# In a two-block kernel's second block, VectorE makes the weights' low parts, ScalarE the high parts and the MLP's squares

## The chip, the cores and the metric

The kernel runs on one core of one Trainium2 chip. The metric is the device time of one execution, in microseconds. The kernel before takes 1734.81 us, the median of 3 runs (1733.33 to 1739.93).

## The reference

256 tokens of width 1024, all in fp32, pass through two blocks. The first has two layers: a gated linear attention and an mLSTM, each followed by a mixture of 16 experts. The change leaves it alone. The second block, cut to its core:

```python
c_act = silu(c)
for l in range(2):
    ada = c_act @ w_ada[l] + b_ada[l]                 # 1024 x 6144: six modulation vectors
    sh1, sc1, gt1, sh2, sc2, gt2 = split(ada, 6)
    h = rms(x, g_mix[l]) * (1 + sc1) + sh1
    parts = split(h @ w_in[l], IN_SPLITS)             # q, k, v of both attentions, and two gates
    y_a = gqa_attention(rope(rms(qa)), rope(rms(ka)), va) @ w_branch_a[l]      # 8 heads over 2
    y_b = dilated_attention(rope(rms(qb)), rope(rms(kb)), vb) @ w_branch_b[l]  # 3 groups of 4 heads
    mixed = sigmoid(gate_a) * y_a + sigmoid(gate_b) * y_b
    x = x + gt1 * (mixed @ w_out[l])
    h2 = rms(x, g_mlp[l]) * (1 + sc2) + sh2
    x = x + gt2 * (square(relu(h2 @ w_ff1[l])) @ w_ff2[l])     # 1024 -> 4096 -> 1024
```

## The kernel before, in words

**Split weights.** A product in fp32 is made of three matmuls: a matrix is split into a high part (`hi`, a cast to a shorter format) and a low part (`lo`, the matrix less its high part), and TensorE adds high by high, high by low and low by high. Activations are split the same way, once (`X_H` and `X_L`; in the MLP `fh` and `fl`). The weights come from HBM in units of 1 MB; half a unit is a chunk of 128 x 1024, and `split` (L349 to L365) makes one chunk's `hi` and `lo`. It is called `LOOK` = 2 chunks ahead of the chunk that TensorE multiplies by (`ahead`), and there are 4 buffers of each kind. A few chunks are split earlier, at the end of a stage (`early`), with `lo` on GpSimd.

**Who makes what.** The Python program that writes the instructions carries a planner. `Clock` (L107) keeps an estimated time of each engine and the estimated end of everything read or written; its cost table (`Timed.cost`) gives each operation a duration by engine and size, and knows nothing of one engine slowing another. `Either` takes, of two engines, the one whose estimated end is earlier, after a handicap: `AV` chooses ScalarE or VectorE (0.0); `VG` VectorE or GpSimd, with GpSimd taken where it would end less than 0.5 us after VectorE; `VG2` the same two, with GpSimd taken only where it would end over 1.0 us earlier. Before the change `hi` goes by `AV`, `lo` by `VG`. Each engine then works off its own instructions in the order in which the program wrote them.

**The second block, layer by layer.** The input projection is followed by the attentions: heads normalised and rotated (`norm_rope`; the result is `xs`, and the small powers of the norms, `hss`, are GpSimd's), scores, softmax, values. The branch projections and gates give `mixed`, transposed and split. The output projection (`out_proj`, L649) works through 128 of the 256 tokens first (mt=0), then the other 128. After each half and 512 columns `emit` (L2300) multiplies by `gt1` (`res`), adds to the residual (`h`), and takes ScalarE's sum of squares (`aff_q`). With a half done, the norm for the MLP starts in the background: `th` is the modulated norm, `X_H` and `X_L` its parts. The MLP (`mlp`, L2317) goes in 8 blocks of 512 hidden columns. `dense_T` leaves a block transposed in PSUM, `square_T` (L2331) makes the relu (`r`), its square, and `fh` and `fl`, two pieces of 128 x 512 for each block; the first block takes another way (`up`, `turn`; there `fl` is taken from PSUM, `fl<-tp,fh`). `down` multiplies the block before by `w_ff2`.

**The modulation columns.** `ada_cols` (L1848) is a generator that runs in the background of other stages, a step at each tick. For each layer it makes 12 groups of 512 columns; each group takes 4 loads of 512 KB (`ada_w`, two buffers). For a load, ScalarE scales one half by `c` (`ada_t`), VectorE multiplies and adds the other half (the load's buffer is then free, and the next load goes out), and from the second load on an addition joins it to the group's sum. After the fourth, VectorE transposes and reduces (`part`), and TensorE finishes with four tiny matmuls (`bgp<-part,fold`), which are taken from a list of hooks at certain places. Two things hold the generator back: a schedule by chunks (`CB`), and `calm` (L1944), which puts a step off, up to ten times, while the planner's clock has the step's engine over 0.9 us later than TensorE. `ada_need(l, 9)` in `emit`, called at the end of the first token half, makes sure that the group 9 is done, the last one that the MLP's norm uses: it takes hooks and ticks until it is.

All operations are recorded by one helper, so that every row of the profile has the line L175; operations are told apart by their tiles.

Of the kernel before, what the change touches and what calls it, by code (L numbers as in the profile page):

```python
# [26 lines left out]
F32 = mybir.dt.float32  # L27
# [3 lines left out]
AF = mybir.ActivationFunctionType  # L31
OP = mybir.AluOpType
# [195 lines left out]
def tile_model(ctx: ExitStack, tc: tile.TileContext, I, out, stages=None, h_in=None):  # L228
    nc = tc.nc
    clock = Clock()  # L230
    PE, V, A, G = [Timed(clock, e, n) for e, n in
                   ((nc.tensor, "PE"), (nc.vector, "V"), (nc.scalar, "A"), (nc.gpsimd, "G"))]
    SP = Timed(clock, nc.sync, "D")
    copies = {("V", "copy"): "tensor_copy"}
    VG, AV = Either((V, G), -0.5), Either((A, V), 0.0, copies)
    VG2 = Either((V, G), 1.0)
# [31 lines left out]
    class Stream:  # L268
# [80 lines left out]
        def split(self, i):  # L349
            u, half = self.chunks[i]  # L350
            shape = self.units[u][0]
            while u not in self.tiles:
                B.tick()
            t = self.tiles[u]
            n = shape[1] // 2
            src = t[:, half * n:half * n + n]
            src = src.rearrange("p k n -> p (k n)")
            hi = clock.slot("hi", 4, hl.tile([P, 1024], F32R, name="hi", tag="hi"))
            lo = clock.slot("lo", 4, hl.tile([P, 1024], F32R, name="lo", tag="lo"))
            AV.copy(hi, src)  # L360
            (G if self.pool else VG).tensor_tensor(lo, src, hi.bitcast(F32), op=OP.subtract)
            self.ready[i] = (hi, lo)
            if half:
                self.tiles.pop(u)
                self.free(u)  # L365
# [651 lines left out]
    def moe_front(l, space):  # L1017
# [99 lines left out]
        def front(mt, nb, rs, norm):  # L1117


            if nb == 0:  # L1120
                if mt == 0:

                    A.activation(R["top0"], c_ones[:, 0:1], AF.Sigmoid)
                B.push(first(mt), True)
            elif mt == 0:
                B.push(later(rs, norm), True)
            else:
                B.drain()
                split(0)
                part(1, 1)  # L1130
                norm()
                logits(1, 1)
                for _ in sigmoids(1, rs):
                    pass
                split(1)
# [1181 lines left out]
    def mlp(l, x, mp):  # L2317
# [13 lines left out]
        def square_T(pq, f):  # L2331
            for i in range(2):
                yield
                r = mp.tile([P, 2, T], F32, name="r", bufs=2)
                A.activation(r, pq[i], AF.Relu)
                VG2.tensor_tensor(r, r, r, op=OP.mult)
                k = slice(2 * i, 2 * i + 2)
                AV.copy(f.hi[:, k], r)
                VG2.tensor_tensor(f.lo[:, k], r, f.hi[:, k].bitcast(F32), op=OP.subtract)

        def turn(r, f):
            yield 1
# [34 lines left out]
        for fb in range(8):  # L2377
            f = XT(mp.tile([P, 4, T], F32R, name="fh", bufs=2), mp.tile([P, 4, T], F32R, name="fl", bufs=2))
            if fb:
                B.push(square_T(dense_T(x), f), True)  # L2380
            else:
                B.push(turn(up(fb), f), True)
            if fb == 6:
                B.push(ada_row(l, 1, gt, 1.0), True)
            if fb:
                down(fb - 1, fx[-1])
            fx.append(f)
# [35 lines left out]
    src = h_in if h_in is not None else I["x"][0]  # L2423
# [240 lines left out]
```

## Time and profile before

| of the profiled execution | |
|---|---|
| span | 1732.9 us |
| its own device time | 1734.7 us |
| TensorE busy (PE) | 1576.5 us, 91% |
| weight loads (PEld) | 1136.3 us, 66% |
| VectorE busy (DVE) | 1112.8 us, 64% |
| ScalarE busy (ACT) | 574.2 us, 33% |
| GpSimd busy (POOL) | 395.3 us, 23% |
| `lo` on GpSimd | 104, mean 2548 ns |
| `lo` on VectorE | 204, mean 1287 ns |
| `hi` on ScalarE | 207, mean 1050 ns |

The second block lies between about 860 and 1720 us. The first layer's output projection adds its residual (`res`) from 1076 to 1088 us, its MLP from 1293 us on; in the second layer the two lie at 1518 to 1528 us and at the end, 1721 us. The attentions' heads come at the start of each layer, round 885 and 1335 us. An engine's busy time is the sum of its instructions' durations, and an instruction that is slowed down by another engine counts with its longer duration. "PEclk" is the clock that TensorE was granted, as a share of the full 2.4 GHz; its other level is 1.2 GHz. "mean ns of one" is a group's mean, and what stands behind the bar is the time in which the engine was idle ahead of the group's instructions, with what ended most of it.

### The profile page before, as it was taken

To read this page: it belongs to the slowest core of one execution; us is meant where nothing else is said; L and a number is where in the kernel's file an instruction comes from. 1 tells how busy PE (TensorE), PEld (TensorE's weight loads), DVE (VectorE), ACT (ScalarE), POOL (GpSimd) and SP (SyncE) were. 2 spreads that over 40 slices of the span, in tenths; PEclk is the share of its full clock that TensorE was granted. 3 is DMA by queue.
4 is the path that set the end of the run, shared out by engine and by line. 5 is a ranking of instruction groups with operands and counts; after the bars stand their busy time and mean duration, and the time that the engine had idled before them with its cause. 6 is when DMAs were issued, how large, how long until landed. Compare 5 with 4: busy or idle time off the path is not lost.

```text
span 1732.9 us, 22647 instructions
## 1 busy us (share of the span) xinstructions
PE 1576.5 (91%) x8772; PEld 1136.3 (66%) x8774; DVE 1112.8 (64%) x1728; ACT 574.2 (33%) x973; POOL 395.3 (23%) x256
## 2 busy tenths in 40 slices
PE   7998999898998799989788998888998889989997
PEld 5865444336776544433466897778986679878996
DVE  4876113106887611121498979898889987779875
ACT  5223111105543211201344453533434544352210
POOL 1232000001333100000364324432125531222110
PEclk9998999898999899999998999999998999999999
DMA  9746999999755589999653676577764446547651
GB/s 321 284 149 229 360 392 411 391 360 238 240 190 194 198 322 373 409 406 387 208 179 110 196 202 221 171 250 257 250 240 152 158 138 179 191 137 241 194 180 41
DMA packets 165770, 422.43 MB, mean 244 GB/s; under 512 B 13017, under 2 KB 14193, under 8 KB 154642
## 3 DMA queue, kind: packets, MB, share of 16 engines
q1 hardware_dynamic: 165458, 420.75, 69.7%
q8 instruction: 73, 1.20, 0.3%
q14 instruction: 47, 0.39, 0.1%
q0 software_dynamic: 192, 0.10, 0.0%
HBM read 419.77 MB, written 1.05 MB: 243 GB/s over the span
## 4 chain that ended last, share of the span: by engine, by line
PE 27%; DVE 12%; issue 6%; ACT 2%; POOL 2%; DMA 1%; DVEq 0%; POOLq 0%; ACTq 0%
PE mm L175 16%; PE acc L175 7%; DVE ada_t L175 3%; DVE lo L175 2%; POOL lo L175 2%; PE sb L175 1%; DVE xs L175 1%; DMA ada_w<-in_w_ada 1%; DVE ro L175 1%; DVE rt L175 1%; ACT pa L175 1%; ACT hi L175 1%; DVE h L175 1%; DVE mx L175 1%; DVE hss L175 1%
## 5 line engine op out<-in xcount | busy, mean ns | idle before, releaser
L175 POOL TENSOR_TENSOR lo<-w,hi 128x1024 fp32r<-128x1024 f32 x104 | 264.4, 2548 | 505.7 <-ACT hi L175 495.9
L175 DVE TENSOR_TENSOR lo<-w,hi 128x1024 fp32r<-128x1024 f32 x204 | 261.4, 1287 | 21.2 <-ACT hi L175 15.3
L175 ACT CAST hi<-w 128x1024 fp32r<-128x1024 f32 x207 | 214.6, 1050 | 146.9 <-PE mm L175 99.9
L175 PE MATMUL mm<-hi,X_H 128*128 128x512 f32 x512 | 221.1, 432 | 29.8 <-ACT X_H L175 15.6
L175 PE MATMUL mm<-lo,X_H 128*128 128x512 f32 x512 | 210.5, 411 | 3.5 <-DVE lo L175 3.2
L175 PE MATMUL mm<-X_H,hi 128*128 128x256 f32 x704 | 206.0, 293 | 1.6 <-ACT raw L175 1.1
L175 PE MATMUL mm<-hi,X_L 128*128 128x512 f32 x512 | 197.4, 409 | 4.8 <-DVE X_L L175 4.7
L175 PE MATMUL mm<-X_L,hi 128*128 128x256 f32 x704 | 201.5, 286 | 0.0
L175 PE MATMUL mm<-X_H,lo 128*128 128x256 f32 x704 | 201.3, 286 | 0.0
L175 PE MATMUL up<-w,X 128*64 128x512 f32 x672 | 194.0, 599 | 0.8 <-ACT X L175 0.8
L175 PEld LDWEIGHTS mm<-hi,X_H 128*128 128x128 f32 x512 | 102.7, 201 | 61.5 <-issue 21.2
L175 PEld LDWEIGHTS mm<-X_H,hi 128*128 128x128 f32 x704 | 136.8, 194 | 4.0 <-ACT raw L175 1.3
L175 PEld LDWEIGHTS mm<-X_L,hi 128*128 128x128 f32 x704 | 137.0, 195 | 0.4
L175 PEld LDWEIGHTS mm<-X_H,lo 128*128 128x128 f32 x704 | 136.8, 194 | 0.0
L175 DVE SCALAR_TENSOR_TENSOR y<-dn,gsl,y 128x512 fp32r<-128x512 f32 x32 | 24.0, 751 | 162.0 <-ACT y L175 162.0
L175 POOL TENSOR_TENSOR ln_rs<-ln_rs,mhalf 128x1 f32<-128x1 f32 x8 | 4.9, 614 | 515.5 <-DVE ln_rs L175 515.5
L175 PEld LDWEIGHTS up<-w,X 128*64 128x64 f32 x672 | 58.7, 138 | 96.8 <-issue 93.0
L175 PEld LDWEIGHTS mm<-hi,X_L 128*128 128x128 f32 x512 | 100.7, 198 | 31.3 <-DVE X_L L175 8.5
L175 PEld LDWEIGHTS mm<-lo,X_H 128*128 128x128 f32 x512 | 102.8, 201 | 24.8 <-DVE lo L175 5.8
L175 PE MATMUL up<-wh,X 128*64 128x512 f32 x336 | 116.2, 604 | 0.0
L175 PE MATMUL dn<-w,hTt 128*64 128x512 f32 x336 | 105.3, 631 | 2.1 <-ACT hTt L175 2.1
L175 DVE TENSOR_TENSOR hb<-sa,up 128x512 f32<-128x512 f32 x16 | 11.0, 687 | 141.1 <-PE up L175 141.1
(412 smaller groups left out, 2953.2 us busy)
## 6 DMA issues: line engine op xcount, KB each, us to landing
w<-in_moe_w SPq DMA_DIRECT2D x126, 1024.0 KB, 9.8
w<-in_w_ff SPq DMA_DIRECT2D x64, 1024.0 KB, 5.5
wh<-in_moe_w SPq DMA_DIRECT2D x124, 512.0 KB, 11.5
ada_w<-in_w_ada SPq DMA_DIRECT2D x96, 512.0 KB, 4.2
w<-in_w_in SPq DMA_DIRECT2D x40, 1024.0 KB, 5.5
w<-in_mlstm_w_in SPq DMA_DIRECT2D x16, 1024.0 KB, 19.9
w<-in_gla_w_in SPq DMA_DIRECT2D x12, 1024.0 KB, 9.8
w<-in_w_out SPq DMA_DIRECT2D x8, 1024.0 KB, 6.1
```

Source lines behind the costliest of these rows:

```text
L175: r = f(*args, **kw)
```

## The change

In the second block (a unit's last field is 2), a chunk's `hi` is always ScalarE's and its `lo` always VectorE's, apart from the `lo` of `early`, which stay on GpSimd. In `square_T` the square becomes an activation of ScalarE, the high part `fh` a cast of ScalarE, and the low part `fl` VectorE's. The planner's cost table and handicaps stay as they are; since it now books these operations on other engines, its later choices and the background generator's steps fall differently.

```diff
--- before.py
+++ after.py
@@ -357,8 +357,9 @@
             src = src.rearrange("p k n -> p (k n)")
             hi = clock.slot("hi", 4, hl.tile([P, 1024], F32R, name="hi", tag="hi"))
             lo = clock.slot("lo", 4, hl.tile([P, 1024], F32R, name="lo", tag="lo"))
-            AV.copy(hi, src)
-            (G if self.pool else VG).tensor_tensor(lo, src, hi.bitcast(F32), op=OP.subtract)
+            late = self.units[u][4] == 2
+            (A if late else AV).copy(hi, src)
+            (G if self.pool else V if late else VG).tensor_tensor(lo, src, hi.bitcast(F32), op=OP.subtract)
             self.ready[i] = (hi, lo)
             if half:
                 self.tiles.pop(u)
@@ -2333,10 +2334,10 @@
                 yield
                 r = mp.tile([P, 2, T], F32, name="r", bufs=2)
                 A.activation(r, pq[i], AF.Relu)
-                VG2.tensor_tensor(r, r, r, op=OP.mult)
+                A.activation(r, r, AF.Square)
                 k = slice(2 * i, 2 * i + 2)
-                AV.copy(f.hi[:, k], r)
-                VG2.tensor_tensor(f.lo[:, k], r, f.hi[:, k].bitcast(F32), op=OP.subtract)
+                A.copy(f.hi[:, k], r)
+                V.tensor_tensor(f.lo[:, k], r, f.hi[:, k].bitcast(F32), op=OP.subtract)
 
         def turn(r, f):
             yield 1
```

VectorE's order in the first layer's output projection, from before the change. `part` is the reduction of a modulation group, `adac` and `mod` its use, `res` and `h` the residual of `emit`.

```order
L175 STREAM_TRANSPOSE ada_t<-ada_t 128x512
L175 TENSOR_REDUCE part<-ada_t 128x16
L175 SCALAR_TENSOR_TENSOR ada_t<-ada_w,ccol,ada_t 128x512
L175 TENSOR_TENSOR adac<-raw,bada 128x4
L175 COPY mod<-adac 128x8
L175 SCALAR_TENSOR_TENSOR mod<-adac,gcol 128x8
L175 TENSOR_TENSOR lo<-w,hi 128x1024
L175 TENSOR_TENSOR res<-mm,gt 128x512
L175 TENSOR_TENSOR h<-h,res 128x512
```

The same place after the change:

```order
L175 STREAM_TRANSPOSE ada_t<-ada_t 128x512
L175 TENSOR_REDUCE part<-ada_t 128x16
L175 TENSOR_TENSOR res<-mm,gt 128x512
L175 TENSOR_TENSOR h<-h,res 128x512
L175 COPY raw<-bgp 128x4
L175 TENSOR_TENSOR adac<-raw,bada 128x4
L175 SCALAR_TENSOR_TENSOR ada_t<-ada_w,ccol,ada_t 128x512 x2
L175 TENSOR_TENSOR ada_t<-ada_t 128x512
L175 SCALAR_TENSOR_TENSOR ada_t<-ada_w,ccol,ada_t 128x512
L175 TENSOR_TENSOR ada_t<-ada_t 128x512
L175 SCALAR_TENSOR_TENSOR ada_t<-ada_w,ccol,ada_t 128x512
L175 TENSOR_TENSOR ada_t<-ada_t 128x512
```

Before, the group that the norm needs (`part`, `adac`, `mod`) is through ahead of the first `res`; after, most of its partial products, its transposition and its `part` come behind the first half's residual. On TensorE, the same projection before, with the tiny matmuls of one group (x4) among those of the weights:

```order
L175 MATMUL mm<-hi,X_H 128x512
L175 MATMUL mm<-lo,X_H 128x512
L175 MATMUL mm<-hi,X_L 128x512
L175 MATMUL bgp<-part,fold 32x4 x4
L175 MATMUL mm<-hi,X_H 128x512
L175 MATMUL mm<-lo,X_H 128x512
```

And after, with those of two groups in a row (x8), at the end of the first half:

```order
L175 MATMUL mm<-hi,X_H 128x512
L175 MATMUL mm<-lo,X_H 128x512
L175 MATMUL mm<-hi,X_L 128x512
L175 MATMUL bgp<-part,fold 32x4 x8
L175 MATMUL mm<-hi,X_H 128x512
L175 MATMUL mm<-lo,X_H 128x512
```

The matmuls of the two groups have moved together, in front of the second half. In the first MLP, VectorE's order before, round one block's `square_T`:

```order
L175 TENSOR_TENSOR r<-r 128x512
L175 CAST fh<-r 128x512
L175 TENSOR_TENSOR fl<-r,fh 128x512
L175 TENSOR_TENSOR r<-r 128x512
L175 CAST fh<-r 128x512
L175 TENSOR_TENSOR fl<-r,fh 128x512
L175 TENSOR_TENSOR lo<-w,hi 128x1024
L175 CAST hi<-w 128x1024
L175 TENSOR_TENSOR lo<-w,hi 128x1024
```

And after:

```order
L175 TENSOR_TENSOR ada_t<-ada_t 128x512
L175 TENSOR_TENSOR fl<-r,fh 128x512
L175 TENSOR_TENSOR lo<-w,hi 128x1024
L175 TENSOR_TENSOR fl<-r,fh 128x512
L175 TENSOR_TENSOR lo<-w,hi 128x1024
L175 SCALAR_TENSOR_TENSOR ada_t<-ada_w,ccol,ada_t 128x512
L175 TENSOR_TENSOR lo<-w,hi 128x1024
```

Of the block's own work only the two `fl` are left on VectorE, and between them stand `lo` of chunks that GpSimd made in part before.

## Rows read from the trace of the kernel before

**Rows 1.** Busy time of each engine by stretch; first line: the columns.

```profile
core 0: us, PE busy (x) PEld busy (x) DVE busy (x) ACT busy (x) POOL busy (x), PEclk, DMA share, GB/s
860.00:965.00 105.00, 89.59 (x420) 68.63 (x420) 92.36 (x172) 48.80 (x110) 57.32 (x50) 0.90 0.47 155
1105.00:1210.00 105.00, 94.18 (x610) 85.49 (x609) 93.70 (x97) 46.31 (x63) 37.14 (x14) 0.93 0.73 246
1320.00:1405.00 85.00, 71.90 (x347) 55.76 (x346) 75.65 (x144) 39.07 (x92) 42.81 (x30) 0.92 0.42 138
1575.00:1700.00 125.00, 125.00 (x824) 114.69 (x824) 103.85 (x109) 23.44 (x31) 19.15 (x9) 1.00 0.58 188
```

**Rows 2.** TensorE's waits, 1085 to 1400 us: in total, times, longest.

```profile
PE mm L175 <- ACT X_H L175: 10.0, 2, 6.0
PE bgp L175 <- DVE part L175: 5.5, 2, 3.4
```

**Rows 3.** VectorE's groups by form, 1100 to 1285: count, busy, mean ns, idle before.

```profile
L175 DVE TENSOR_TENSOR lo<-w,hi 128x1024 fp32r<-128x1024 f32 x38 | 48.6, 1280 | 6.5 <-ACT hi L175 5.7
L175 DVE SCALAR_TENSOR_TENSOR ada_t<-ada_w,ccol,ada_t 128x512 f32<-128x512 f32 x29 | 29.5, 1023 | 2.1 <-ACT ada_t L175 2.0
L175 DVE TENSOR_TENSOR ada_t<-ada_t 128x512 f32<-128x512 f32 x21 | 20.9, 993 | 0.7
L175 DVE TENSOR_TENSOR fl<-r,fh 128x512 fp32r<-128x512 f32 x14 | 20.5, 1466 | 0.5
L175 DVE TENSOR_TENSOR r<-r 128x512 f32<-128x512 f32 x14 | 14.5, 1036 | 1.1 <-ACT r L175 1.1
L175 DVE TENSOR_TENSOR fl<-tp,fh 128x512 fp32r<-128x512 f32 x2 | 1.4, 691 | 2.3 <-ACT fh L175 2.3
```

**Rows 4.** Timeline of GpSimd and VectorE round 1068: start, duration.

```profile
1068.03 6.28 POOL L175 TENSOR_TENSOR lo<-w,hi 128x1024 fp32r<-128x1024 f32 x2 [6.37 <-ACT hi L175]
...
1069.15 2.89 DVE L175 TENSOR_TENSOR ada_t<-ada_t 128x512 f32<-128x512 f32 x1
```

**Rows 5.** TensorE's waits, 860 to 965, then 960 to 1085.

```profile
PE mm L175 <- DVE xs L175: 4.0, 1, 4.0
...
PE mm L175 <- DVE th L175: 3.6, 2, 1.8
```

**Rows 6.** Groups by form, 860 to 965 (two), then 1320 to 1405.

```profile
L175 POOL TENSOR_TENSOR lo<-w,hi 128x1024 fp32r<-128x1024 f32 x10 | 24.3, 2434 | 10.8 <-ACT hi L175 10.8
...
L175 DVE CAST hi<-w 128x1024 fp32r<-128x1024 f32 x4 | 2.7, 687 | 0.0
...
L175 POOL TENSOR_TENSOR lo<-w,hi 128x1024 fp32r<-128x1024 f32 x9 | 21.8, 2430 | 6.6 <-ACT hi L175 6.6
```

**Rows 7.** Timeline of VectorE, then ScalarE, in the first output projection.

```profile
1072.08 0.71 DVE L175 STREAM_TRANSPOSE ada_t<-ada_t 128x512 f32<-128x512 f32 x1
1077.64 0.74 DVE L175 SCALAR_TENSOR_TENSOR ada_t<-ada_w,ccol,ada_t 128x512 f32<-128x512 f32 x1
1078.42 0.69 DVE L175 TENSOR_TENSOR ada_t<-ada_t 128x512 f32<-128x512 f32 x1
...
1074.95 0.72 ACT L175 ACTIVATE ada_t<-ada_w,ccol 128x512 f32<-128x512 f32 x1
1077.76 0.63 ACT L175 ACTIVATE aff_q<-h 128x512 f32<-128x512 f32 x1 [2.08 <-DVE h L175]
```

**Rows 8.** The tile `ada_w`, 1040 to 1110: its loads.

```profile
DMA to landing us min/median/max: 3.6/3.8/6.0
```

**Rows 9.** Waits of the whole span: in total, times, longest.

```profile
ACT ada_t L175 <- DMA ada_w<-in_w_ada: 59.0, 25, 7.4
```

**Rows 10.** ScalarE's groups by form, 1100 to 1285.

```profile
L175 ACT CAST hi<-w 128x1024 fp32r<-128x1024 f32 x44 | 45.7, 1046 | 40.3 <-PE mm L175 26.6 <-PE acc L175 12.1 <-issue 1.3
L175 ACT ACTIVATE ada_t<-ada_w,ccol 128x512 f32<-128x512 f32 x30 | 21.5, 720 | 28.5 <-DMA ada_w<-in_w_ada 26.0 <-DVE ada_t L175 2.4
L175 ACT ACTIVATE r<-r 128x512 f32<-128x512 f32 x2 | 1.3, 632 | 0.1
```

## The prediction

> **What bounds the kernel now.** I began with the page's busy shares (TensorE 91%, VectorE 64%, ScalarE 33%, GpSimd 23%), which mix two blocks; only the second, from about 860 us on, is changed. So next the same columns by stretch [rows 1]. There the reader is to see three kinds of stage. In the last MLP (1575 to 1700) TensorE is busy 125.00 of 125 us at full clock: nothing can be gained. At the head of both attentions (860 to 965, 1320 to 1405) and in the first half of the first MLP (1105 to 1210) TensorE idles 15.4, 13.1 and 10.8 us, at granted clocks of 0.90, 0.92 and 0.93, while VectorE is busy for 88 to 89% of the time. The other columns leave ScalarE under half. Third, the list of waits says for whom TensorE idles there: in the MLP for `part`, VectorE's reduction of a modulation column [rows 2]; in the attention for `xs`, VectorE's normalised heads [rows 5]. These are latenesses of VectorE, whose queue is in order: whatever is slow in it delays all behind it. The gaps in front of the MLPs and of the second attention, where TensorE waits up to 6.0 us for ScalarE's `X_H` [rows 2], are chains of dependent steps and stay out of the sum.
>
> **Why VectorE is late.** The rows of the first MLP, by form, show it [rows 3]. The same subtraction of 128x512 takes 0.691 us as `fl<-tp,fh`, with one operand in PSUM, and 1.466 us as `fl<-r,fh`, with both in SBUF. The timeline shows one such case: GpSimd has two `lo` from 1068.03 on, for 6.28 us together, and the VectorE addition that starts at 1069.15 takes 2.89 us, where the same one alone took 0.69 [rows 4, 7]. So a GpSimd `lo` holds up a VectorE instruction that starts beside it. The price per GpSimd `lo`, from the means less the lone duration: 29 x (1.023 - 0.74) = 8.2, 21 x (0.993 - 0.69) = 6.4, 14 x (1.466 - 0.691) = 10.9, 14 x (1.036 - 0.69) = 4.8; together 30.3 us beside 20 of them [rows 3, 7], 1.5 us each. VectorE makes a `lo` itself in 1.28 us. Moving one from GpSimd to VectorE is therefore a small gain for VectorE, not a load.
>
> The Trainium skill ("Perfetto Trace Analysis", section Optimizing Scalar/DVE Operations) says that with VectorE saturated, handing work to ScalarE or even GpSimd may make sense, though the two share a read port, so that an exchange between them may not help. Its first half speaks against this change, its second for it: by the first alone VectorE gets its 70 `lo` back for nothing, and by the rows it gives up more than it takes on. The first half is the last rival below.
>
> **What the change does to each engine.** Only the order of the instructions decides this, and it shows the edit does what it says: VectorE's casts `hi` fall from 101 to 19, its `lo` rise from 204 to 274, GpSimd's `lo` fall from 104 to 34, and 27 squares and 27 casts `fh` leave VectorE for ScalarE. ScalarE pays 82 x 1.05 for the casts, 28 x 0.632 for the squares [rows 10], and about as much for `fh`: some 120 us over 860, on an engine that is under half busy. That is costed at nothing; its cover is that idle half, and the price without it is the second-last rival.
>
> First MLP: VectorE loses 30.3 us of collisions, 14 `hi` and 14 squares at 0.69 (19.3) [rows 6, 7] and the 14 casts `fh` (not even counted), and gains 20 x 1.28 = 25.6: 24 us less in the 185 us of rows 3. It is then no longer late for `part`. TensorE there can win back its 10.8 us idle and 0.07 x 105 = 7.4 us of clock [rows 1], 18.2 at most. What is late next is ScalarE's wait for `ada_w`, which feeds the same columns, so I take **15** (bounds 5 to 18).
>
> Heads of the attentions: 10 and 9 GpSimd `lo` go [rows 6]. VectorE: -15.0 + 12.8 - 4 x 0.69 = -5.0 us, and, with as many `hi`, -13.5 + 11.5 - 2.8 = -4.8. GpSimd's small powers `hss`, which every head norm waits for, also no longer stand behind a `lo` of 2.43 us. A stage that VectorE bounds shortens by about what VectorE sheds; with the powers I take **7** each. Bounds: 0, if these are chains of latency whose work is beside the point (VectorE's new `lo` can hold up a power as a GpSimd `lo` held up VectorE; 12 powers behind 1.28 us each would eat 15), and 26 or 20, if all idle time and all clock loss goes (15.4 + 0.10 x 105; 13.1 + 0.08 x 85).
>
> Output projection of the second layer and the attention tails: some steps of VectorE and ScalarE change places, two `th` additions go to GpSimd; nothing on either side, within 3 us.
>
> **What the change adds.** The planner's clock now sees a busier VectorE, and holds back the background work on the modulation columns. The order shows the consequence in the first layer's output projection: before, TensorE's multiplication `bgp` for the last column that the MLP needs stands inside the first token half; now two of them stand together behind that half, and the rest of the projection is queued behind them. On VectorE the four partial products of the second column come after the residual of that half. From the end of the half TensorE thus waits for one chain [rows 7, 8]: `res` and `h`, additions of 0.69 each, ScalarE's square 0.63, two `ada_t` activations 1.44, VectorE's product 0.74, the load into the buffer that this frees 3.8, activation 0.72, product 0.74, addition 0.69, transposition 0.71, and a reduction taken as long: 11.6 us, 12 with the hand-overs. The load ranges from 3.6 to 6.0, so 11.5 to 14. The clock will fall with such a gap: the 10.8 us of gaps in the first MLP went with 7.4 us of it. Most of one long gap is spent at low clock without cost, so +2 for what runs behind it. Of the 3.6 us that TensorE waits for `th` in this stage now [rows 5] some 2 should go with VectorE's lateness. Sum: **+12** (bounds 6 to 18).
>
> **Sum.** -15 - 7 - 7 + 12 = -17 us on the profiled execution's 1734.7 us, which is its span of 1732.9 and 1.8 around it, and within 0.2 us of the median shown (1734.81). Forecast 1718 us. What this kernel can tell from no change is about 0.5%, 8.7 us: faster is below 1726, slower above 1743.5.
>
> **The rivals.**
> - The attention heads give all they can. Then GpSimd's `lo` was the whole cause of TensorE's idling there, and the sum is -18 - 26 - 20 + 12 = -52: 1683; taken at 1690, as not every step will go. For it: the longest waits of TensorE in these stages, as the 4.0 us of [rows 5], end on VectorE. Against: the softmax and the norm are chains of five and more steps each. 0.13.
> - The attention heads give nothing, being chains; the MLP's 15 and the projection's 12 nearly cancel: 1732. For it: VectorE stays over 80% busy there. 0.16.
> - ScalarE in order. ScalarE waits 59.0 us for `ada_w` in 25 waits, up to 7.4 us each, and 26.0 of that lies in the first MLP [rows 9, 10]. Before, VectorE took the `hi` that fell into such a wait; now all stand behind it. Place: the first MLP. TensorE is ahead by the two chunks split in advance; a chunk is 24 or 12 matmuls, 18 on the mean, and 824 of them take 125 us [rows 1], so a wait decides from 5.5 us on, which the longest passes. Should each wait reach TensorE whole, the 26 us come in place of the 15 won: 1734.7 - 14 + 12 + 26 = 1759. Against: those waits are themselves VectorE's lateness, since the next load goes out only when VectorE has read the buffer. 0.09.
> - GpSimd's help was real: VectorE's slow instructions have another cause than GpSimd, the 70 `lo` are a net load, only the casts and squares compensate (70 x 1.28 = 90 against 82 x 0.69 + 27 x 0.69 = 75 and the `fh`), and nothing is won anywhere: 1734.7 + 12 = 1747. Against: rows 3 and 4. 0.05. This is what the first half of the rule from the Trainium skill, named above, would make of it.
>
> **How the numbers follow.** Forecast 0.57, with a range of its own from 1705 to 1729. Faster: 0.57 and 0.13, and 0.01 of the third case, 0.71. Same: the rest of the chains, 0.15. Slower: 0.14. The range leaves out half of the first rival below and nearly all of the slower two above: 1688 to 1738.
>
> **What would show it.** Right: no GpSimd `lo` in the second block but the six that are made early; `fl<-r,fh` at 0.7 us; VectorE busy for some 80% between 1105 and 1210, without TensorE's waits for `part` there; attention heads shorter by 5 to 9 us each; one new TensorE gap of 11 to 14 us before `bgp` in the first output projection, the only place that gets longer. Wrong: `fl` still at 1.4 us (the collision was something else); TensorE waiting for ScalarE's `hi` in the MLPs; the attention heads as long as now; or the gap before `bgp` above 18 us.

## The result, and the profile after

The changed kernel takes 1690.54 us (median of 4 runs, 1689.23 to 1691.40) against 1734.38 us of the kernel before in the same runs: a ratio of 0.9737, 95% interval 0.9720 to 0.9755. That is 43.8 us less. The forecast was 17 us less: the direction was right, the size less than half of what came. 1690 us is the number that the first rival gave, at a chance of 0.13; whether for its reason is looked at below.

The span fell from 1732.9 to 1687.3 us. Where, is found by taking the same matmul in both traces and subtracting its start times:

| stretch of the kernel before, us | what it is | forecast | measured |
|---|---|---|---|
| 860 to 965 | attention heads, first layer | -7 | -14.2 |
| 965 to 1085 | attention tail, output projection to the norm | +12 | +7.0 |
| 1085 to 1105 | norm ahead of the first MLP | 0 | -5.5 |
| 1105 to 1285 | first MLP | -15 | -15.0 |
| 1285 to 1320 | norm ahead of the second layer | 0 | -1.3 |
| 1320 to 1405 | attention heads, second layer | -7 | -9.9 |
| 1405 to 1575 | tail, projection and norm, second layer | 0 | -6.2 |
| 1575 to 1700 | rest of the second MLP | 0 | 0.0 |

The sum is -45.1 us against a forecast of -17; the first block, which isn't changed, is 0.5 us apart. Of the 28.1 us that the forecast lacks, the heads account for 10.1, the stretches that it put at nothing for 13.0, and the row with the new wait for 5.0. First the busy times of the same four pieces of work as in [rows 1] (columns: the stretch and its length, busy us with the count for TensorE, its weight loads, VectorE, ScalarE and GpSimd, then TensorE's granted clock, the DMA share and GB/s):

```profile
860.40:950.40 90.00, 83.83 (x420) 64.24 (x421) 77.98 (x172) 51.49 (x113) 32.24 (x39) 0.98 0.49 159
1091.80:1180.10 88.30, 88.30 (x594) 80.18 (x592) 66.90 (x80) 55.63 (x76) 2.21 (x1) 1.00 0.80 271
1290.50:1365.70 75.20, 69.38 (x346) 53.28 (x345) 66.00 (x145) 42.34 (x97) 23.93 (x22) 0.95 0.47 154
1529.40:1654.40 125.00, 125.00 (x824) 114.61 (x823) 65.69 (x64) 67.27 (x83) 0.00 (x0) 1.00 0.55 182
```

In the first heads the same 420 matmuls are busy for 83.83 us in place of 89.59: the clock rose from 0.90 to 0.98 of the full 2.4 GHz, and that is 5.8 us; TensorE's idle time there fell from 15.4 to 6.2 us, another 9.2. The first half of the first MLP has no idle time and no low clock left. The last MLP shows the opposite: VectorE sheds 38 us of work and ScalarE takes on 44, and TensorE needs 125.00 us as before.

VectorE's groups by form in the first MLP, which answer to [rows 3] (count, busy us, mean ns of one, then the idle time before them and what ended it):

```profile
L175 DVE TENSOR_TENSOR lo<-w,hi 128x1024 fp32r<-128x1024 f32 x58 | 70.9, 1232 | 22.1 <-ACT hi L175 22.1
L175 DVE SCALAR_TENSOR_TENSOR ada_t<-ada_w,ccol,ada_t 128x512 f32<-128x512 f32 x30 | 22.1, 747 | 14.0 <-ACT ada_t L175 14.0
L175 DVE TENSOR_TENSOR ada_t<-ada_t 128x512 f32<-128x512 f32 x20 | 13.8, 689 | 0.4
L175 DVE TENSOR_TENSOR fl<-r,fh 128x512 fp32r<-128x512 f32 x14 | 9.7, 690 | 3.7 <-ACT fh L175 3.7
```

Three groups that took 1023, 993 and 1466 ns take 747, 689 and 690 on the same engine. `fl<-r,fh` with both operands in SBUF is now as fast as `fl<-tp,fh` was. VectorE's own `lo` has 22.1 us of idle time ahead of it, ended by ScalarE's `hi`: VectorE now waits for ScalarE, and TensorE, two chunks behind, doesn't feel it.

TensorE's waits in the output projection and the norm behind it, 1020 to 1100 us (us in total, times, longest), which answer to [rows 2, 5]:

```profile
PE bgp L175 <- DVE part L175: 13.5, 2, 12.6
PE mm L175 <- DVE th L175: 1.6, 1, 1.6
PE mm L175 <- ACT X_H L175: 1.5, 1, 1.5
```

The new wait for `part` is there, 12.6 us at its longest. The timeline of VectorE, then of ScalarE, shows the serial chain inside it (start, duration, operation; in brackets the idle time before it and what ended it):

```profile
1055.93 0.69 DVE L175 TENSOR_TENSOR h<-h,res 128x512 f32<-128x512 f32 x1
...
1059.46 0.69 DVE L175 TENSOR_TENSOR ada_t<-ada_t 128x512 f32<-128x512 f32 x1
1063.47 0.75 DVE L175 SCALAR_TENSOR_TENSOR ada_t<-ada_w,ccol,ada_t 128x512 f32<-128x512 f32 x1 [3.32 <-ACT ada_t L175]
...
1065.94 0.69 DVE L175 TENSOR_TENSOR ada_t<-ada_t 128x512 f32<-128x512 f32 x1
1066.67 0.71 DVE L175 STREAM_TRANSPOSE ada_t<-ada_t 128x512 f32<-128x512 f32 x1
1067.42 0.69 DVE L175 TENSOR_REDUCE part<-ada_t 128x16 f32<-128x512 f32 x1
...
1062.72 0.72 ACT L175 ACTIVATE ada_t<-ada_w,ccol 128x512 f32<-128x512 f32 x1 [4.12 <-DMA ada_w<-in_w_ada]
```

ScalarE waits 4.12 us for a load that could only go out when VectorE had freed its buffer, and VectorE waits 3.32 us for ScalarE.

### The profile page after: what moved, and what is told of

Same layout as the page of the kernel before. It is cut to its first block, busy times and chain, and to the rows that moved or that the text cites. A ratio compares the mean times of both kernels' runs of the same rounds, so it can differ in the third digit from the quotient of the medians.

```text
span 1687.3 us, 22598 instructions
## 1 busy us (share of the span) xinstructions
PE 1556.7 (92%) x8773; PEld 1119.2 (66%) x8774; DVE 977.3 (58%) x1644; ACT 687.9 (41%) x1118; POOL 224.7 (13%) x195
## 3 DMA queue, kind: packets, MB, share of 16 engines
HBM read 419.77 MB, written 1.05 MB: 249 GB/s over the span
## 4 chain that ended last, share of the span: by engine, by line
PE 27%; DVE 12%; ACT 4%; issue 3%; DMA 3%; POOL 1%; ACTq 0%; DVEq 0%; POOLq 0%
PE mm L175 17%; PE acc L175 6%; DVE lo L175 3%; DMA ada_w<-in_w_ada 3%; DVE ada_t L175 2%; ACT hi L175 1%; PE sb L175 1%; ACT pa L175 1%; DVE xs L175 1%; DVE h L175 1%; DVE th L175 1%; DVE aff_t L175 1%; DVE rt L175 1%; DVE X_L L175 0%; DVE hss L175 0%
## 5 line engine op out<-in xcount | busy, mean ns | idle before, releaser
L175 DVE TENSOR_TENSOR lo<-w,hi 128x1024 fp32r<-128x1024 f32 x274 | 342.3, 1258 | 114.3 <-ACT hi L175 113.4
L175 ACT CAST hi<-w 128x1024 fp32r<-128x1024 f32 x289 | 298.2, 1050 | 106.4 <-PE mm L175 64.0
L175 PE MATMUL mm<-hi,X_H 128*128 128x512 f32 x512 | 216.3, 423 | 16.0 <-ACT X_H L175 8.5
L175 PE MATMUL mm<-hi,X_L 128*128 128x512 f32 x512 | 192.8, 400 | 3.6 <-DVE X_L L175 3.5
L175 PEld LDWEIGHTS mm<-hi,X_H 128*128 128x128 f32 x512 | 99.8, 195 | 48.0 <-issue 13.3
L175 PE MATMUL acc<-lo,fh 128*128 128x512 f32 x256 | 100.7, 393 | 0.3 <-DVE lo L175 0.3
L175 PE MATMUL acc<-hi,fl 128*128 128x512 f32 x256 | 100.8, 394 | 0.0
L175 PE MATMUL acc<-hi,fh 128*128 128x512 f32 x256 | 99.6, 389 | 0.0
```

Source lines behind the costliest of these rows:

```text
L175: r = f(*args, **kw)
```

## The experiments

Each time stands beside runs of the kernel before on the same chip (1732 to 1735 us). "Frozen" kernels book every step in the planner as the kernel before does, so that each engine's order and the background's steps are those of before, and only issue the named instructions on another engine. Places are compared by the same matmul, as in the table. They are firmer than the totals: the frozen kernels, whose first block isn't edited, start the second between 4.4 us earlier and 3.3 us later than the kernel before.

**1 and 2. Each edit alone, planner free.** The first has only the edit of `split`, the second only that of `square_T`.

> Only the weights' edit; the MLP's squares and casts as before, and the planner free to reorder. Theory (a GpSimd low part holds up the VectorE instruction beside it, so what counts is that 70 of them leave GpSimd): both attention heads, the gaps before the MLPs and most of the first MLP's gain appear, some 1700 us (1693 to 1708). Rival 1 (VectorE was simply overloaded, and the casts and squares taken off it are the gain): the heads, with 9 casts less only, gain 6 us at most, and the MLP needs the other edit: 1722 or more. Rival 2 (the new order is the gain, not the engines): no number; it is decided by the third and fourth run.

> Only the MLP's edit; weights as before. Theory: only the two MLPs can change; 14 squares of 1.04 and 14 casts leave VectorE in the first MLP, about 20 us of its work, but its low parts beside GpSimd's stay slow: TensorE's waits for the modulation columns shrink by half, 1727 us (1722 to 1733). Rival 1: the first MLP's whole 15 us come from here: 1719 or less.

1693.10 us (0.9771, 0.9743 to 0.9798) and 1724.50 us (0.9948, 0.9924 to 0.9972). The weights' edit alone does what the whole change does, place by place: -14.4 in the first heads, +6.7 in the projection with the same wait, 12.2 us at its longest, -5.4 in the norm ahead of the first MLP, -12.6 in that MLP, -10.4 in the second heads. That refutes its first rival. The MLP's edit alone gains 8.8 us in the first MLP, 1.6 in the first heads, and loses 3.8 in the projection; its time lies within the forecast. The two don't add up.

**3 and 4. The order of before, other engines.** In the fourth:

```diff
-            (G if self.pool else VG).tensor_tensor(lo, src, ...)
+            # booked as VG books it, issued on VectorE
+            (G if self.pool else loV if late else VG).tensor_tensor(lo, src, ...)
```

and in the third `hi`, the squares, `fh` and `fl` likewise go to the engines of the change.

> All substitutions of the change, but the planner books every step as it did before, so that the order of the instructions on TensorE and of the background work is that of before. Theory (engines, not order): the gains stay, and the new wait of 13.5 us before the modulation matmuls in the first output projection is gone, since they stand where they stood: 1681 us (1675 to 1688). Rival 2 (order): without the new order most of the gain is gone, 1715 or more.

> Order and bookings of before; the one thing that differs is that the second block's 70 low parts which GpSimd made are VectorE's. Theory: the interference is most of the gain, though VectorE now carries 90 us more of low parts and still all casts and squares: 1698 us (1688 to 1708). Rival 1 (overload): VectorE is loaded more and TensorE waits longer, 1735 or more.

1692.85 us (0.9758, 0.9722 to 0.9794) and 1689.70 us (0.9759, 0.9727 to 0.9791). The fourth is the main result: 70 subtractions moved from GpSimd to VectorE, no cast and no square taken off VectorE, no order changed, and the time is that of the whole change. A plain overload of VectorE as the cause is out: it got 70 x 1.23 = 86 us of work more, and its busy time on the page still fell, from 1112.8 to 1070.4 us. The rest of the change, added in the third run, gains nothing. My 1681 for the third run was wrong: the new wait is gone as expected (-6.4 in the projection where the change has +7.0), but the heads gain 9.3 in place of 14.2 and the first MLP 5.3 in place of 15.0, with the old waits for `part` of 4.5 and 2.3 us still there. So the new order, which holds the columns' steps back, helps the heads and the MLP by about what the wait costs.

**5 and 6. The interference by itself.** The fourth kernel, and wherever GpSimd had made a low part it now does work that nobody reads:

```diff
+            if late and not self.pool and loV.chose == "G" and scr:
+                for d in range(4):                            # fifth run
+                    n4 = slice(256 * d, 256 * d + 256)
+                    G.eng.tensor_tensor(scr[0], src[:, n4], hi.bitcast(F32)[:, n4], op=OP.subtract)
+                # sixth run: one column subtracted, then eight times G.eng.memset(scr[0], 0.0)
```

> The fourth run's kernel (order of before, all low parts on VectorE), and at each place where GpSimd made a low part, GpSimd now subtracts the same operands into a scratch tile that nobody reads (four pieces of 128x256), so that nothing waits for it. Theory (GpSimd's reading holds VectorE up): the loss comes back though GpSimd's result isn't needed; VectorE's all-SBUF instructions are slow again and carry the low parts besides: 1735 us (1725 to 1755). Rival (what was late was the low part from GpSimd, 2.4 us where VectorE takes 1.25): the scratch work costs nothing, 1690.

> As the run before, but the scratch work is a tiny subtraction of one column, so that it comes at the same time, and eight fills of the scratch tile with zero, which read nothing. Theory: a fill that reads nothing doesn't hold VectorE up, or far less; the powers of the head norms stand behind it as they stood behind the low parts. 1692 us (1688 to 1700). Rival (the queue of GpSimd, in which the powers wait, is the cost in the heads): the heads lose 6 us or more each, 1702 or more.

1765.03 us (1.0177, 1.0150 to 1.0205) and 1695.18 us (0.9766, 0.9735 to 0.9796). Scratch subtractions cost 75.3 us against the fourth run, scratch fills 5.5, at or near the noise. The groups in the first MLP, first of the fifth run, then of the sixth:

```profile
L175 DVE TENSOR_TENSOR ada_t<-ada_t 128x512 f32<-128x512 f32 x21 | 18.5, 881 | 0.7
L175 DVE TENSOR_TENSOR r<-r 128x512 f32<-128x512 f32 x14 | 13.9, 993 | 0.6 <-ACT r L175 0.6
L175 DVE TENSOR_TENSOR fl<-r,fh 128x512 fp32r<-128x512 f32 x14 | 13.5, 963 | 0.5
L395 POOL TENSOR_TENSOR scr<-w,hi 128x256 bf16<-128x256 f32 x78 | 90.6, 1161 | 104.1 <-issue 50.2 <-ACT hi L175 49.0
```

```profile
L175 DVE TENSOR_TENSOR ada_t<-ada_t 128x512 f32<-128x512 f32 x22 | 15.2, 691 | 0.7
L175 DVE TENSOR_TENSOR fl<-r,fh 128x512 fp32r<-128x512 f32 x14 | 9.7, 692 | 0.5
L395 POOL MEMSET scr<- 128x256 bf16 x159 | 52.9, 333 | 9.2
```

The fills keep GpSimd busy for 53 us there, as long as its low parts did before (52.4), and leave VectorE's instructions at 691 and 692 ns; the subtractions make the same instructions 881 and 963. So it isn't GpSimd's being busy that holds VectorE up, nor that its low part came late. What the subtractions do and the fills don't is read whole tiles from SBUF. The Trainium skill ("SBUF — State Buffer", section Who interferes with whom) says as much: a VectorE instruction with two SBUF inputs contends with a GpSimd instruction that reads SBUF, not with one that only writes it. These two runs agree on both halves. My 1735 for the fifth was too low: the four pieces take 1.05 us each over the block, 4.2 us where one `lo` took 2.4, so they probably hold VectorE longer than what they stand for. The sixth also bounds GpSimd's queue: the heads' powers stand behind fills and the heads lose 2.9 and 1.7 us, not the 6 of the rival.

**7 to 9. Taking the new wait away.** `calm` puts a step off while an engine is over 0.9 us later than TensorE by the planner's clock. The seventh kernel raises the 0.9 to 4.0; the eighth also gives VectorE the six `early` low parts; the ninth raises it to 8 from the 34th to the 56th weight chunk only, behind the heads.

> The changed kernel, with the one threshold that puts a step of the modulation columns off raised from 0.9 to 4.0 us of the planner's clock; the matmuls of the group that the norm needs then stand inside the first token half again. Theory (the new wait of 13.5 us is the planner's holding back, no lack of engine time): the wait goes, and as the heads get some of that work back, 5 to 10 us of it are won: 1683 us (1678 to 1688). Rival (the columns are late because of the loads): the wait stays, 1690.

> As the run before, and the six early low parts of the second block are VectorE's as well. Theory: four of them stand beside the residual and the norm ahead of the MLPs, where diag takes 2.4 us in place of 0.29 and one h 1.9 in place of 0.69: 2 to 5 us less than the run before, 1680. Rival: VectorE makes them 1.25 us each in the same short chain, nothing is won.

> The changed kernel with the threshold raised to 8 us, but only from the 34th to the 56th weight chunk after the second block's first, that is behind the attention heads, where VectorE is busy for 73% of the time; the heads keep their 0.9. The order then has the matmuls of the group that the norm needs inside the first token half. Theory (the heads can't bear the columns' steps, the stretch behind them can): the wait of 13.5 us goes and the heads keep their gain: 1680 us (1675 to 1686). Rival (what the heads gave back with the threshold of 4 comes from elsewhere, or the steps are late wherever they go): 1690 or more.

1708.28 (0.9842, 0.9814 to 0.9871), 1710.31 (0.9846, 0.9823 to 0.9869) and 1698.31 us (0.9788, 0.9771 to 0.9804): three misses; in the ninth its rival came true. The wait before `bgp` went each time, and more was paid elsewhere. In the seventh the first heads are 13.3 us longer than in the changed kernel. Their busy times (columns as above), and TensorE's waits there:

```profile
862.40:965.90 103.50, 87.13 (x419) 66.34 (x420) 88.75 (x186) 55.70 (x119) 34.36 (x42) 0.93 0.54 177
```

```profile
PE mm L175 <- DVE xs L175: 4.9, 2, 3.0
```

VectorE has 14 instructions more than the 172 of the changed kernel, 88.75 us of work against 77.98, and the clock is back at 0.93. In the ninth the heads keep their gain (-0.2 against the changed kernel), and the wait moves behind the half's residual:

```profile
PE tpd L175 <- DVE diag L175: 7.7, 1, 7.7
```

The timeline of VectorE ahead of it, and one row of ScalarE, tell why:

```profile
1081.13 0.75 DVE L175 SCALAR_TENSOR_TENSOR ada_t<-ada_w,ccol,ada_t 128x512 f32<-128x512 f32 x1 [2.64 <-ACT ada_t L175]
...
1083.99 0.68 DVE L175 TENSOR_TENSOR res<-mm,gt 128x512 f32<-128x512 f32 x1
...
1080.37 0.72 ACT L175 ACTIVATE ada_t<-ada_w,ccol 128x512 f32<-128x512 f32 x1 [3.40 <-DMA ada_w<-in_w_ada]
```

Steps of the next group, which nothing needs yet, stood ahead of `res` and waited for their load.

**10 to 12. The rest alone; the first block; the low parts alone, planner free.** The tenth is frozen: ScalarE makes `hi`, squares and `fh`, GpSimd keeps its 70 `lo`. The eleventh is the ninth with the first block's `lo` on VectorE too; 24 of GpSimd's 28 there go, its four `early` ones stay. The twelfth is the change with `lo` alone.

> Order and bookings of before; ScalarE makes the casts, the squares and the fh of the second block, but GpSimd keeps its 70 low parts. With the run that moved only the low parts this splits the change in two. Theory: little, 1728 us (1720 to 1735), since every VectorE instruction beside a low part is still held up. Rival 1 (overload): VectorE has 96 us less to do, so 1715 or less.

> As the first run of this batch, and the low parts of the first block are VectorE's too (28 fewer on GpSimd). Theory: there the weights' loads and the experts set the time, VectorE waits for most of it, so what it is held up costs little: 0 to 5 us less than the first run. Rival: the interference costs there as in the second block, 1.5 us and more each: 30 us less.

> Only the low parts go to VectorE; the casts stay with whichever of ScalarE and VectorE the planner picks, the MLP's squares as before, and the planner is free. Theory: as the changed kernel, 1691 us (1686 to 1697), stall before the modulation matmuls included. Rival (the casts on ScalarE are needed once the planner is free): 1700 or more.

1717.30 (0.9903, 0.9868 to 0.9938), 1700.59 (0.9798, 0.9780 to 0.9816) and 1695.82 us (0.9762, 0.9735 to 0.9789). The tenth gained 17 us, between what theory and overload had said: taking work off VectorE does count for something while the interference stays, 7.9 us of it in the first MLP. But in the heads VectorE is busy for 2.7 us less than in [rows 1], 89.62 against 92.36, and the stage is only 1.0 us shorter. The frozen fourth kernel there, first, and the tenth:

```profile
856.50:949.00 92.50, 83.08 (x420) 64.48 (x421) 83.66 (x181) 48.50 (x109) 33.19 (x39) 0.98 0.52 170
```

```profile
859.00:963.00 104.00, 88.30 (x422) 67.69 (x423) 89.62 (x169) 52.85 (x114) 56.98 (x49) 0.93 0.46 152
```

With the low parts gone from GpSimd the stage takes 92.5 us at a clock of 0.98; with the casts gone, and VectorE down to 169 instructions, 104.0 for the same work and two matmuls more. In the first block the 24 cost nothing that could be seen. The twelfth confirms the fourth without freezing.

**13 to 15. What was still open.** The thirteenth raises the threshold to 8 only for the groups up to the needed one and holds the next group back; the fourteenth moves every second of the 70 `lo`, the fifteenth the 27 of the input projections' weights (both frozen).

```diff
+            while n == 10 and S.chunk_at < first["l0"] + 58:
+                yield
+            slack[0] = 8.0 if n < 10 and S.chunk_at >= first["l0"] + 34 else 0.9
```

> The changed kernel; the threshold is 8 us only for the groups up to the needed one and only from the 34th weight chunk of the block on, and the next group, which nothing needs soon, is held until the 58th. In the ninth run it was that next group's steps that stood ahead of the residual on VectorE and ScalarE and turned the wait of 13.5 us into others. Theory (the heads' gain and the wait can be had apart): 1682 us (1677 to 1687). Rival (the wait also hides the norm's chain, and the steps of the columns have to be paid for somewhere on the path): 1690 or more.

> Order and bookings of before; every second of the 70 low parts goes from GpSimd to VectorE, 35 in all. If each that goes is worth the same, half of the 45 us: 1712 us (1707 to 1718). Rival (a stage gains only when VectorE is clear of the last one, so the price is not by piece): 1722 or more; or, if the first ones taken were the ones that counted, 1702 or less.

> Order and bookings of before; only the low parts of the two input projections' weights, 27 of the 70, go from GpSimd to VectorE. Theory: the attention heads gain by themselves what they gained with all 70 moved, 11.7 and 9.5 us, and nothing else moves: 1712 us (1707 to 1717). Rival (the heads' gain is work that the rest of the block took over): the heads gain less than half of that, 1725 or more.

1688.19 (0.9735, 0.9694 to 0.9775), 1715.85 (0.9887, 0.9855 to 0.9918) and 1707.72 us (0.9841, 0.9810 to 0.9872). Half of the pieces give 19.6 us by the ratios, nearly half of the 41.8 of all 70, as forecast. But that isn't a price by the piece. In the fourteenth run's trace the heads, with about half of their pieces gone, gain 1.8 and 3.6 us, where all gave 11.7 and 9.6; the first MLP, with half of its pieces gone, gains 9.3, where all gave 7.2. In the heads the rival is nearer, and the half in the total is partly luck. The 27 of the input projections give 27.6 us, about 1.0 each, so the other 43 are worth about 0.3 each, within intervals of some 5 us; in the fifteenth run's trace the heads gain 9.2 each and the second block 21. The thirteenth falls between its theory and its rival. It has no wait before `bgp` and isn't shown to be faster than the changed kernel; its steps are paid in smaller waits of the same projection and the norm behind it:

```profile
PE mm L175 <- DVE lo L175: 5.9, 5, 2.6
PE mm L175 <- DVE th L175: 2.1, 1, 2.1
PE mm L175 <- ACT X_H L175: 2.0, 1, 2.0
```

**16 and 17. The rest of GpSimd's reading.** The thirteenth, with the planner barred from GpSimd in the second block (both handicaps set to 1e6), and then with the six `early` low parts on VectorE too.

> The run of the thirteenth kernel's order rules, and from the second block on the planner may no longer choose GpSimd at all: the additions of the columns, of th and of the head rotation that it still gave away (some 20) are VectorE's. Theory: each of them held VectorE up as a low part did, for its shorter time; 2 to 6 us less than the thirteenth: 1684 us (1680 to 1688). Rival (what is left of GpSimd's work now runs beside idle time of VectorE, and the heads, which VectorE bounds, get more to do): 1689 or more.

> As the run before, and the six early low parts are VectorE's too, so that in the second block GpSimd only makes powers and the head tables. Theory: the norm ahead of each MLP loses the hold-ups of diag (2.4 us against 0.29) and of one h: 2 to 4 us less than the run before. Rival, as in the eighth run: nothing.

1684.02 (0.9726, 0.9693 to 0.9759) and 1689.94 us (0.9755, 0.9725 to 0.9785). The sixteenth has the lowest median of all, but its interval overlaps those of the thirteenth and of the change, so it isn't shown to be faster than either. In the one trace of each, its second block gains 52.4 us where the change's gains 45.1, so part of this may be real. The six early low parts gained nothing in either place, the eighth run and the seventeenth. That they still hold an instruction of the norm up is visible in the changed kernel (GpSimd, then VectorE):

```profile
1480.10 2.37 POOL L175 TENSOR_TENSOR lo<-w,hi 128x1024 fp32r<-128x1024 f32 x1
```

```profile
1480.13 2.42 DVE L175 TENSOR_SCALAR diag<-ident,rs 128x128 f32<-128x128 f32 x1 [0.67 <-POOL rs L175]
```

`diag` takes 0.29 us when it is alone. Why its removal isn't worth its 2.1 us was not settled.

## Why the prediction fell short

**The mechanism was right, and it is shown.** GpSimd's `lo` hold VectorE up (fifth and sixth run), and their going is the gain (fourth and fifteenth). `fl<-r,fh` came to 0.69 us as said, and the rival that GpSimd's help was real is refuted by the fourth run. So is ScalarE in its order: TensorE's only wait between 1092 and 1257 us is one of 0.3, for a `lo`, though ScalarE still waits 37.0 us there for `ada_w`.

**The step that failed: the 5.0 us that VectorE was to shed in each of the heads.** VectorE's busy time in the first heads fell by 14.4 us, from 92.36 to 77.98, and in the second by 9.7, from 75.65 to 66.00. The stages became 14.2 and 9.9 us shorter. So "a stage that VectorE bounds shortens by about what VectorE sheds" held here, and what went into it was too small. About 3.6 of the 14.4 are two products and three additions of the modulation columns that the new order moved out. In the fourth run, with the order fixed, VectorE's time still fell by 8.7, although nine `lo` came in at 1.22: the other instructions took 19.7 us less, 2.0 for each of the ten pieces, where the MLP's rows gave 1.5. In the heads the instructions beside a `lo` are short and are held about as long as it runs. In the second layer's heads, before and then after:

```profile
L175 DVE TENSOR_SCALAR pa<-pa,smx 128x256 f32<-128x256 f32 x15 | 8.5, 628 | 0.1
L175 DVE TENSOR_TENSOR xs<-ro,rt 128x256 f32<-128x256 f32 x8 | 7.5, 942 | 0.8 <-DVE rt L175 0.5
L175 DVE TENSOR_SCALAR mx<-mx 128x4 f32<-128x4 f32 x4 | 3.4, 842 | 0.1
```

```profile
L175 DVE TENSOR_SCALAR pa<-pa,smx 128x256 f32<-128x256 f32 x16 | 4.6, 350 | 0.1
L175 DVE TENSOR_TENSOR xs<-ro,rt 128x256 f32<-128x256 f32 x8 | 3.4, 424 | 0.3
L175 DVE TENSOR_SCALAR mx<-mx 128x4 f32<-128x4 f32 x4 | 0.9, 218 | 0.1
```

Of the eight `xs<-ro,rt` before, two took 2.50 and 2.49 us and the others 0.42. The working for the second heads also took "as many `hi`" as in the first, four of 0.69 us; the trace has five, 6.5 us in all.

The clock was left out of the 7, though it was in the bounds: of the first heads' 15.0 us by the stretches above, 9.2 are idle time of TensorE and 5.8 are the same matmuls at a higher clock. And the rule is a rough one. In the tenth run VectorE sheds 2.7 us in the first heads and the stage gains 1.0, in the fourteenth 3.8 and 1.8. A likely reason, which no run isolates, is that a held instruction counts only where it stands in the chain that TensorE waits for.

**"Chains of dependent steps ... stay out of the sum" failed too, and so did the "nothing on either side" for the second layer's projection and tails.** These stretches gave 5.5, 1.3 and 6.2 us. In the second layer 3.8 of the 6.2, and 4.6 of the 5.5 in the fourth run, lie at the start of the output projection, where `mixed` is split. Before, GpSimd's `lo` stood beside that split (GpSimd, then VectorE; below, the same two operations after the change):

```profile
1499.75 7.69 POOL L175 TENSOR_TENSOR lo<-w,hi 128x1024 fp32r<-128x1024 f32 x3 [5.41 <-ACT hi L175]
...
1499.77 2.67 DVE L175 CAST X_H<-th 128x512 fp32r<-128x512 f32 x1
1502.47 2.73 DVE L175 TENSOR_TENSOR X_L<-th,X_H 128x512 fp32r<-128x512 f32 x1
```

```profile
1460.11 0.43 DVE L175 CAST X_H<-th 128x512 fp32r<-128x512 f32 x1
1460.57 0.69 DVE L175 TENSOR_TENSOR X_L<-th,X_H 128x512 fp32r<-128x512 f32 x1
```

A chain of dependent VectorE steps gets shorter when its steps are no longer held. The same place in the first layer (1045 to 1065 us) gains 5.9 us, and 5.6 in the fourth run, inside the row with the new wait. The gap ahead of the first MLP is less clear. In the fourth run, which has no new wait, TensorE waits 6.2 us for `X_H` there as before, so the 5.5 may be the other side of that wait: the norm of the first half ran while TensorE stood before `bgp`. But the thirteenth, which has no such wait either, gains 5.0 there, so this cause stays open.

**The new wait** was forecast at 12 and is 13.5 in two pieces; the stretch with it came out at +7.0, since the same projection's waits for `th` and `X_H` fell from 5.6 to 1.6 us and the tail gained 2.2. With the 5.5 behind it, the two rows together lose 1.5 us. That the change would be some 10 us faster without it, as I then expected, was not borne out by the seventh, ninth and thirteenth kernels.

**The first MLP** gained exactly the 15 of the forecast, in part by luck. With the order frozen it gains 5.3 (third run) and 7.2 (fourth), with waits for `part` of 6.8 and 5.4 us left; the rest comes with the new order, in which TensorE no longer waits for `part` there. That was not in the working.

**The first rival's 1690** came true in its number, not in its working: it let both heads give everything, 46 us, and they gave 24. That it was near is luck.

A faster kernel than the changed one was not shown; several can't be told from it, the shortest edit among them being the low parts alone (twelfth run).

## What to carry to other kernels

Before a helper engine is credited with the work that it takes over, compare the same instruction of the busy engine with and without the helper beside it, in the stage at hand: here each helper's subtraction of 2.4 us cost the helped engine 1.5 to 2.0 us, more than doing it itself at 1.23. Price a hold-up by how long the other instruction runs, not by the mean of a stage with long instructions, and add the clock that a gap takes with it. A background task that is moved away from a tight stage comes back somewhere else; look at the sum of both places before removing the wait that it leaves.

## What the runs showed of the hardware

Zero fills of 128x256 on GpSimd, mostly 0.31 us each, some 2.6 us for eight in a row, left VectorE's subtraction of two SBUF tiles untouched (692 ns in the run with fills, 693 without); reading subtractions of the same tile size made it 963. The hold-up is mutual: the fifth run's pieces take 0.73 us with hardly any VectorE work beside them and up to 1.78 with VectorE's own `lo`. It also takes in VectorE instructions with one tensor in SBUF, however small: `diag` of 128x128, with a scalar beside it, went from 0.29 to 2.42 us, and the cast of 128x512 above from 0.43 to 2.67. "Who interferes with whom" in the Trainium skill's "SBUF — State Buffer" counts such instructions among those that can take the shared port.
